# The gate-and-up product of an encoder trunk: seven block products in another order, two of them continued in PSUM, and weight parts made by pairs of row tiles

## The chip, the cores and the metric

The kernel runs on one core of a Trainium2 chip. Times are device microseconds of one launch of the whole program. Three runs of the kernel before gave 1506.62, 1507.06 and 1509.12 us; the median is 1507.06 us.

## The reference, cut to what matters

The reference is a trunk of two layers for 512 tokens with a model width of 1024. Each layer has a mixer and a SwiGLU feed-forward block with 2816 hidden columns, each followed by a residual and a LayerNorm. All of it is float32. The change touches only the first product of the feed-forward block, which is computed once in each of the two layers:

```
def swiglu_ffn(x, w_gate_up, w_down):
    gu = x @ w_gate_up                       # (512, 1024) @ (1024, 2 * 2816)
    gate, up = gu[..., :FFN_HIDDEN], gu[..., FFN_HIDDEN:]
    return (jax.nn.silu(gate) * up) @ w_down
```

## The kernel before, in words

A float32 operand is held in two parts, a high one (a rounded copy, type fp32r) and a low one (the operand less its high part). `split` (L185) makes them: ScalarE casts the high part (L186) and VectorE, or GpSimd where told, subtracts for the low part (L187). A product of two operands takes three matmuls: high by high (L180), high of x by low of the weights, and low of x by high of the weights (L181 and L182); `gemm3` issues them one behind the other. The profile writes the operands of a matmul as out<-moving or stationary names; "wl" is the weights' low part.

`ffn` (L1112) computes x @ w_gate_up by Winograd's form of Strassen's product. x^T is cut in halves of the tokens (256) and of the model's columns (512), w_gate_up in halves of its rows and in gate and up. Seven block products P1 to P7 take the place of eight. The blocks of x (P1 to P7's left operands) and their parts are made once, by `sink` (L1132), when the norm before hands over x^T; P1, P2, P4 and P7 take parts of x^T itself, P5, P6 and P3 take sums of its blocks from the tile S.

The hidden columns are worked in six groups, four of 512 columns and two of 384 (`GROUPS`, L35). For one group the weights are four blocks B11, B12 (gate and up of the upper rows), B21, B22 (of the lower rows), each of four row tiles of 128 rows. They are loaded by eight DMAs on SyncE's queue, one for a row tile with gate and up side by side (L1192, 512 KB). GpSimd makes the blocks' sums (`sub`, L1200): for P6, B11 <- B12 - B11 and T2 <- B22 - B11; for P5 the new B11 serves; for P7, B12 <- B22 - B12; for P4, T2 <- B21 - T2.

`product` (L1156) runs one block product for a group: for each of two pairs of row tiles it takes a set of places for parts (tags wh and wl, two sets), and for each row tile of the pair it calls `split` on that tile (128 x 512 or 128 x 384) and then six matmuls, three for each half of the block's tokens (u = 0, 1). So a product has 24 matmuls, four casts and four low parts, and ends in two PSUM banks. There are eight banks: four with tag g, one each with t and o, two with s for transposes; the products take g, g, and t with o in turn.

`step` (L1223) runs a product and takes its result out of PSUM. P1 is copied by ScalarE (s1, L1239). All others are added by VectorE (L1234): g = P2 + s1; u = P6 + s1; w = P5 + u; v = P7 + w; u = P7 + u; w = P3 + w; u = P4 + u. ScalarE applies silu to g (L1246) and to u (L1255), GpSimd multiplies w by g (L1252), and VectorE multiplies v by u (L1256). So w and v are the two token halves of the hidden layer; `turn` (L1258) transposes them on TensorE (L1263) into the rows of `hid`, which ScalarE copies from PSUM (L1264).

`work` (L1269) runs the groups one behind the other in the order P1 P2 P6 P5 P7 P3 P4. The transposes of a group come after P2 of the next one. The first product of group 1 (`first_product`, L1174) is taken ahead and stands behind P2 of group 0, since the second half of the tokens is still in the norm then. `LOW` (L954) says which engine makes the low parts of these three products: VectorE and GpSimd in turn for the first layer's P1, GpSimd for all in the second layer.

The order in which each engine gets its instructions isn't that of the program text alone: a planner hands each engine, by a model of the times, the earliest instruction in program order whose operands and places are ready. Each engine then runs its queue in that order.

What follows the product is the down projection (`down`, L1655, with `down_ln`), which is unchanged; it uses the same two sets wh and wl and the same buffers w for its weights.

## Time and profile before

| | |
|---|---|
| median of the runs | 1507.06 us (1506.62 to 1509.12) |
| profiled execution, its span | 1508.2 us |
| TensorE busy | 1390.2 us, 92% |
| VectorE busy | 1113.9 us, 74% |
| ScalarE busy | 646.3 us, 43% |
| GpSimd busy | 532.1 us, 35% |
| mean granted TensorE clock | 0.964 |

The profiled execution's own time is its span, from the first to the last instruction; nothing outside it is recorded. Engines are named PE (TensorE's matmuls), PEld (its weight loads), DVE (VectorE), ACT (ScalarE), POOL (GpSimd) and SP (SyncE). In a timeline, a start in us is followed by the time to the end of a run of like instructions; a bracket holds the idle time ahead of it and who ended it. Matmuls are pipelined: the start of one to the start of the next is their rate, while the duration shown holds the latency too.

### The profile page before, as it was taken

To read this page: it belongs to the slowest core of one execution; us is meant where nothing else is said; L and a number is where in the kernel's file an instruction comes from. 1 tells how busy PE (TensorE), PEld (TensorE's weight loads), DVE (VectorE), ACT (ScalarE), POOL (GpSimd) and SP (SyncE) were. 2 spreads that over 40 slices of the span, in tenths; PEclk is the share of its full clock that TensorE was granted. 3 is DMA by queue.
4 is the path that set the end of the run, shared out by engine and by line. 5 is a ranking of instruction groups with operands and counts; after the bars stand their busy time and mean duration, and the time that the engine had idled before them with its cause. 6 is when DMAs were issued, how large, how long until landed. Compare 5 with 4: busy or idle time off the path is not lost. (4 is left out here: it accounts for less than half of the span.)

```text
span 1508.2 us, 22040 instructions
## 1 busy us (share of the span) xinstructions
PE 1390.2 (92%) x8366; PEld 1090.2 (72%) x8366; DVE 1113.9 (74%) x1858; ACT 646.3 (43%) x1223; POOL 532.1 (35%) x422
## 2 busy tenths in 40 slices
PE   8989989999959888999999999999988988989997
PEld 4767767667737676788877877766666776888886
DVE  3688776446697889889556457988798788988456
ACT  5533233344334444445433246555433444455341
POOL 1433122131384576466501230000466377561000
PEclk9999999999979999999999999999999999999999
DMA  5212111203503203222233221111403212222222
GB/s 178 82 50 49 35 43 40 51 22 119 181 15 140 83 29 112 85 84 66 88 99 113 91 67 60 51 52 45 169 25 125 99 32 93 84 84 85 85 97 98
DMA packets 57051, 120.98 MB, mean 80 GB/s; under 512 B 19312, under 2 KB 20464, under 8 KB 56816
## 3 DMA queue, kind: packets, MB, share of 16 engines
q1 hardware_dynamic: 56416, 117.46, 23.4%
q10 hardware_dynamic: 528, 2.10, 0.4%
q8 instruction: 66, 1.08, 0.3%
q14 instruction: 41, 0.34, 0.1%
HBM read 116.58 MB, written 2.95 MB: 79 GB/s over the span
## 5 line engine op out<-in xcount | busy, mean ns | idle before, releaser
L187 DVE TENSOR_TENSOR wl<-w,wh 128x512 fp32r<-128x512 f32 (+3 forms) x289 | 270.5, 968 | 72.2 <-ACT wh L186 72.0
L186 ACT CAST wh<-w 128x512 fp32r<-128x512 f32 (+3 forms) x309 | 195.0, 665 | 205.6 <-PE ps_g L182 143.9
L181 PE MATMUL ps_g<-wl,xh 128*128 128x512 f32 (+1 forms) x432 | 174.9, 405 | 37.9 <-DVE wl L187 35.1
L208 POOL TENSOR_TENSOR wl<-w,wh 128x512 fp32r<-128x512 f32 x64 | 88.1, 1379 | 246.0 <-ACT wh L207 213.5
L180 PE MATMUL ps_g<-wh,xh 128*128 128x512 f32 (+1 forms) x432 | 170.3, 396 | 3.0 <-ACT wh L186 2.4
L182 PE MATMUL ps_g<-wh,xl 128*128 128x512 f32 (+1 forms) x432 | 170.2, 396 | 0.0
L1200 POOL TENSOR_TENSOR w<-w 128x512 f32<-128x512 f32 (+1 forms) x96 | 145.3, 1528 | 30.8 <-DVE wl L187 28.2
L181 PEld LDWEIGHTS ps_g<-wl,xh 128*128 128x128 f32 x432 | 85.9, 199 | 65.3 <-DVE wl L187 48.0
L180 PE MATMUL ps_g<-xh,wh 128*128 128x512 f32 (+2 forms) x296 | 117.2, 396 | 0.0
L187 DVE TENSOR_TENSOR wl<-tt,wh 128x512 fp32r<-128x512 f32 (+1 forms) x96 | 104.1, 1116 | 17.6 <-ACT wh L186 17.5
L181 PE MATMUL ps_g<-wl,ah 128*128 128x512 f32 x288 | 112.2, 391 | 2.9 <-DVE wl L187 2.9
L181 PE MATMUL ps_g<-xl,wh 128*128 128x512 f32 (+2 forms) x296 | 114.8, 388 | 0.0
L182 PE MATMUL ps_g<-xh,wl 128*128 128x512 f32 (+2 forms) x296 | 114.6, 387 | 0.0
L181 PE MATMUL ps_g<-wl,Sh 128*128 128x512 f32 (+1 forms) x288 | 110.5, 384 | 3.5 <-DVE wl L187 3.4
L180 PE MATMUL ps_g<-wh,Sh 128*128 128x512 f32 (+1 forms) x288 | 110.2, 385 | 3.3 <-ACT wh L186 3.3
L182 PE MATMUL ps_g<-wh,al 128*128 128x512 f32 x288 | 112.0, 390 | 0.0
L180 PE MATMUL ps_g<-wh,ah 128*128 128x512 f32 x288 | 110.8, 392 | 0.2
L182 PE MATMUL ps_g<-wh,Sl 128*128 128x512 f32 (+1 forms) x288 | 109.0, 378 | 0.0
L180 PEld LDWEIGHTS ps_g<-wh,xh 128*128 128x128 f32 x432 | 85.8, 199 | 18.2 <-ACT wh L186 2.6
L187 DVE TENSOR_TENSOR al<-hid,ah 128x512 fp32r<-128x512 f32 x72 | 50.3, 710 | 62.8 <-ACT ah L186 62.7
L182 PEld LDWEIGHTS ps_g<-wh,xl 128*128 128x128 f32 x432 | 86.4, 200 | 12.2
L187 POOL TENSOR_TENSOR wl<-w,wh 128x512 fp32r<-128x512 f32 (+1 forms) x20 | 32.8, 1656 | 176.0 <-ACT wh L186 176.0
(433 smaller groups left out, 3151.5 us busy)
## 6 DMA issues: line engine op xcount, KB each, us to landing
w<-in_w_gu SPq DMA_DIRECT2D x64, 512.0 KB
w<-in_w_dn SPq DMA_DIRECT2D x44, 512.0 KB
w<-in_w_even SPq DMA_DIRECT2D x48, 256.0 KB
w<-in_w_gu SPq DMA_DIRECT2D x32, 384.0 KB
w<-in_w_q SPq DMA_DIRECT2D x12, 384.0 KB
w<-in_w_eo SPq DMA_DIRECT2D x16, 256.0 KB
w<-in_w_mi SPq DMA_DIRECT2D x8, 512.0 KB
w<-in_w_mo SPq DMA_DIRECT2D x8, 512.0 KB
```

Source lines behind the costliest of these rows:

```text
L180: nc.tensor.matmul(out, lhsT=wh, rhs=xh, start=first, stop=False)
L181: nc.tensor.matmul(out, lhsT=wh, rhs=xl, start=False, stop=False)
L182: nc.tensor.matmul(out, lhsT=wl, rhs=xh, start=False, stop=last)
L186: c = nc.scalar.copy(h, src)
L187: (eng or nc.vector).tensor_tensor(l, in0=src, in1=h, op=ALU.subtract)
L208: nc.gpsimd.tensor_tensor(l, in0=w, in1=h, op=ALU.subtract)
L1200: nc.gpsimd.tensor_tensor(o, in0=a, in1=b, op=ALU.subtract)
```

## The change

The seven products of a group are no longer run one group at a time. P1 of a group (but group 1, whose P1 is still taken ahead, now between P1 and P2 of group 0) comes before P4 of the group before, and P2 after it. P2's matmuls go on in the banks of P1 (tags t and o) without clearing them, and P4's in those of P7 (two of the four banks g); so g = silu of those banks, and u + P7 is no more added by itself. Group 1's P2 has banks of its own. `product` calls `split` once for a pair of row tiles (128 x 1024, or 128 x 768) and issues all matmuls with the pair's high part, then those with its low part. In groups 0 to 3, but for the first three products, each third pair takes its parts from a third set, in the places of hid's tiles 4 and 5. The weights are loaded by blocks, four DMAs for each, one for a row tile's half (256 KB or 192 KB); the first block goes into the buffers w of the down projection, all others into four buffers of one block each. The scratch blocks of `sink` move from hid's tiles 3 and 4 to 2 and 3.

```diff
-LOW = ("PDPD", "DDDD", "DDDD"), ("PPPP", "PPPP", "PPPP")
+LOW = ("PD", "DD", "DD"), ("PP", "PP", "PP")
...
-    full = [{n: hid.row(12 + 4 * u + i).rearrange("p (k t) -> p k t", t=P) for i, n in enumerate(("P1", "P2", "P7", "P6"))} for u in range(2)]
+    full = [{n: hid.row(8 + 4 * u + i).rearrange("p (k t) -> p k t", t=P) for i, n in enumerate(("P1", "P2", "P7", "P6"))} for u in range(2)]
...
+    def parts(n, spare):
+        count[0] += 1
+        if spare and count[0] % 3 == 0:
+            if not third:
+                third.extend(hid.make(4 + r, "third", F32R).rearrange("p m s -> p (m s)") for r in range(2))
+            hl = third
+        else:
+            hl = [g.wp.tile([P, 1024], F32R, tag=t, name=t, bufs=2) for t in ("wh", "wl")]
+        return [x[:, :2 * n].rearrange("p (q n) -> p q n", q=2) for x in hl]
+
+    def banks(chain):
+        return [g.pp.tile([P, S], F32, tag=t, name="ps_g", bufs=4 if t == "g" else 1) for t in ("to" if chain else "gg")]
+
+    def product(name, n, source, acc, first=True, spare=True, eng="DD"):
+        A_ = A[name]
         for k2 in range(2):
-            h, l = (g.wp.tile([P, 1024], F32R, tag=t, name=t, bufs=2) for t in ("wh", "wl"))
-            for q in range(2):
-                k = 2 * k2 + q
-                qs = slice(512 * q, 512 * q + n)
-                split(nc, h[:, qs], l[:, qs], source(k), nc.gpsimd if eng[k] == "P" else nc.vector)
-                for u in range(2):
-                    us = slice(P * u, P * u + P)
-                    gemm3(nc, acc[u], A_[0][:, k, us], A_[1][:, k, us], h[:, qs], l[:, qs], k == 0, k == 3)
-        return acc
+            h, l = parts(n, spare)
+            split(nc, h, l, source(k2), nc.gpsimd if eng[k2] == "P" else nc.vector)
+            for b, w in enumerate((h, l)):
+                for q in range(2):
+                    k = 2 * k2 + q
+                    for u in range(2):
+                        for a in range(2 - b):
+                            nc.tensor.matmul(acc[u][:, :n], lhsT=A_[a][:, k, P * u:P * u + P], rhs=w[:, q], start=first and k + a + b == 0,
+                                             stop=k + b == 4, skip_group_check=True)
...
+        def load(r, q):
+            if (r, q) == (0, 0) and j != 1:
+                b = [g.wp.tile([P, 1024], F32, tag="w", name="w", bufs=2)[:, :2 * n].rearrange("p (k n) -> p k n", k=2) for k2 in range(2)]
+            else:
+                t = tp.tile([P, 2048], F32, tag="raw", name="raw", bufs=4)[:, :4 * n].rearrange("p (k n) -> p k n", k=4)
+                b = [t[:, 0:2], t[:, 2:4]]
+            for k in range(4):
+                nc.sync.dma_start(b[k // 2][:, k % 2], w[4 * r + k][:, q * n:q * n + n])
+            out[r, q] = b
...
+            chained = {"P2": "P1", "P4": "P7"}.get(name)
+            if chained in acc:
+                acc[name] = acc[chained]
+            else:
+                acc[name] = banks(name in ("P1", "P2") and not (j == 1 and name == "P1"))
+                chained = None
+            product(name, n, lambda k2: source(name, k2), acc[name], chained is None, spare, eng)
...
+                elif name == "P2":
+                    if chained:
+                        d.g = E("g")[:, :n]
+                        nc.scalar.activation(d.g, acc[name][u][:, :n], AF.Silu)
+                    else:
+                        d.g = add(name, u, d.s1)
+                        nc.scalar.activation(d.g, d.g, AF.Silu)
...
                 elif name == "P7":
-                    d.v = add("v", d.w)
-                    add(d.u2, d.u2)
+                    d.v = add(name, u, d.w)
...
+        for j, x in enumerate(gs):
+            more = j < 4
+            if j != 1:
+                x.step("P1", more and j > 0, LOW[i][0] if j == 0 else "DD")
+            if j == 0:
+                gs[1].step("P1", False, LOW[i][1])
+            else:
+                gs[j - 1].turn(0)
+                gs[j - 1].step("P4", more)
+                for r, q in ((1, 0), (0, 1), (1, 1)):
+                    x.load(r, q)
+            x.step("P2", more and j > 0, LOW[i][2] if j == 0 else "DD")
+            if j:
+                gs[j - 1].turn(1)
+            x.step("P6", more)
+            x.step("P5", more)
+            if 0 < j < last:
+                gs[j + 1].load(0, 0)
+            x.step("P7", more)
+            x.step("P3", more)
+        gs[last].step("P4", False)
```

## Rows read from the trace of the kernel before

**Rows 1.** The page's first part: busy time, share of the span, instructions.

```profile
span 1508.2 us, 22040 instructions
...
PE 1390.2 (92%) x8366; PEld 1090.2 (72%) x8366; DVE 1113.9 (74%) x1858; ACT 646.3 (43%) x1223; POOL 532.1 (35%) x422
```

**Rows 2.** Windows: length, busy PE, PEld, DVE, ACT, POOL, clock, DMA share, GB/s.

```profile
425.39:464.87 39.48, 26.41 (x81) 19.32 (x82) 34.88 (x33) 15.95 (x29) 25.82 (x17) 0.68 0.04 14
464.87:703.80 238.93, 218.78 (x1013) 184.48 (x1012) 206.91 (x247) 109.38 (x210) 140.59 (x100) 0.96 0.24 83
1111.79:1138.34 26.55, 17.67 (x73) 12.78 (x72) 26.48 (x29) 15.47 (x28) 19.21 (x13) 0.90 0.11 39
1138.34:1376.32 237.98, 218.14 (x1010) 184.80 (x1011) 206.31 (x247) 107.55 (x206) 140.01 (x96) 0.95 0.23 80
530.27:577.40 47.13, 43.34 (x185) 35.06 (x184) 40.62 (x45) 21.26 (x38) 29.15 (x18) 0.93 0.25 91
```

**Rows 3.** Windows of PE alone: length, busy PE, granted clock, DMA share, GB/s.

```profile
519.38:530.26 10.88, 10.88 (x49) 1.00 0.92 331
691.31:703.78 12.47, 12.47 (x73) 1.00 0.06 18
543.48:549.95 6.47, 6.46 (x16) 0.53 0.00 0
```

**Rows 4.** Timeline of PE, 451 to 554.

```profile
451.25 0.80 PE L181 MATMUL ps_g<-wl,xh 128*128 128x512 f32 x1 [5.54 <-DVE wl L187]
...
539.83 0.39 PE L180 MATMUL ps_g<-wh,xh 128*128 128x512 f32 x1
543.49 0.80 PE L181 MATMUL ps_g<-wl,xh 128*128 128x512 f32 x1 [3.28 <-DVE wl L187]
...
553.06 1.03 PE L1263 MATMUL ps_s<-cst,w 128*128 128x128 f32 x8
553.85 0.48 PE L180 MATMUL ps_g<-wh,Sh 128*128 128x512 f32 x1
```

**Rows 5.** Waits in 464 to 703.8: us in total, times, longest.

```profile
PEld ps_g L181 <- DVE wl L187: 23.3, 22, 3.8
...
PE ps_g L181 <- DVE wl L187: 15.2, 7, 3.4
```

**Rows 6.** Timeline of POOL, 530 to 562.

```profile
530.56 3.00 POOL L1252 TENSOR_TENSOR w<-w,g 128x512 f32<-128x512 f32 x2 [19.49 <-DVE w L1234]
...
537.80 3.42 POOL L1200 TENSOR_TENSOR w<-w 128x512 f32<-128x512 f32 x2
...
554.71 6.47 POOL L1200 TENSOR_TENSOR tt<-w,tt 128x512 f32<-128x512 f32 x4
```

**Rows 7.** Timeline of DVE, 534 to 643.

```profile
534.03 1.28 DVE L187 TENSOR_TENSOR wl<-w,wh 128x512 fp32r<-128x512 f32 x2
...
538.32 3.45 DVE L1256 TENSOR_TENSOR v<-v,u 128x512 f32<-128x512 f32 x2
541.69 5.12 DVE L187 TENSOR_TENSOR wl<-w,wh 128x512 fp32r<-128x512 f32 x3
...
636.09 6.47 DVE L187 TENSOR_TENSOR wl<-w,wh 128x384 fp32r<-128x384 f32 x5
```

**Rows 8.** Groups by form, DVE, 720 to 790: busy, mean ns, idle before.

```profile
L187 DVE TENSOR_TENSOR wl<-w,wh 128x1024 fp32r<-128x1024 f32 x12 | 14.8, 1230 | 2.6 <-ACT wh L186 2.6
```

**Rows 9.** Groups by form, ACT, 720 to 790.

```profile
L186 ACT CAST wh<-w 128x1024 fp32r<-128x1024 f32 x12 | 12.6, 1046 | 0.0
```

**Rows 10.** Groups by form, DVE, 464.87 to 703.8.

```profile
L1234 DVE TENSOR_TENSOR g<-ps_g,s 128x512 f32<-128x512 f32 x6 | 3.8, 676 | 0.0
```

**Rows 11.** Line 187 in the whole trace: ns least, median, most; forms.

```profile
L187 DVE TENSOR_TENSOR wl<-w,wh x289: 424/692/2349, 438.5 to 1469.1; 128x512 fp32r<-128x512 f32 x73, 128x384 fp32r<-128x384 f32 x40, 128x1024 fp32r<-128x1024 f32 x23, 128x768 fp32r<-128x768 f32 x8
...
L187 POOL TENSOR_TENSOR wl<-w,wh x20: 1271/1725/2612, 426.1 to 1128.5; 128x512 fp32r<-128x512 f32 x18, 128x1024 fp32r<-128x1024 f32 x2
```

**Rows 12.** Timeline of SP, 1085 to 1095.

```profile
1087.65 4.28 SPq L1178 DMA_DIRECT2D w<-in_w_gu  x4
```

More of the change, by code (lines that the diff above doesn't have):

```diff
@@ L175, with of @@
 class Ctx:
-    pass
+    @classmethod
+    def of(cls, **k):
+        c = cls()
+        c.__dict__.update(k)
+        return c
 def gemm3(nc, out, wh, wl, xh, xl, first, last):
@@ L1174, in first_product @@
-    def first_product(j):
-        r = [g.wp.tile([P, 1024], F32, tag="w", name="w", bufs=2) for k2 in range(2)]
-        for k in range(4):
-            nc.sync.dma_start(r[k // 2][:, 512 * (k % 2):512 * (k % 2) + 512], g.I[f"w_gu{i}{j}"][k][:, :512])
-        acc = product(A["P1"], 512, lambda k: r[k // 2][:, 512 * (k % 2):512 * (k % 2) + 512], LOW[i][2])
-        out = []
-        for u in range(2):
-            out.append(E("s1"))
-            nc.scalar.copy(out[u], acc[u])
-        return out
@@ L1186, in group @@
-    def group(j, s1=None):
+    third = []
+    count = [0]
+    def parts(n, spare):
[9 more added lines that the diff above has]
+        return [g.pp.tile([P, S], F32, tag=t, name="ps_g", bufs=4 if t == "g" else 1) for t in ("to" if chain else "gg")]
@@ L1187, in group, with blocks @@
+    def blocks(j):
         c, n = GROUPS[j]
         w = g.I[f"w_gu{i}{j}"]
[L1189 to L1196 removed]
@@ L1197, in group @@
-        T2 = [tt[:, k * n:k * n + n] for k in range(4)]
+        out = {}
+        def load(r, q):
[7 more added lines that the diff above has]
+            out[r, q] = b
@@ L1199, in sub, with group, source @@
+        return out, load
+    def group(j):
+        c, n = GROUPS[j]
+        B, load = blocks(j)
+        e = [Ctx(), Ctx()]
+        acc, T2 = {}, []
         def sub(o, a, b):
             nc.gpsimd.tensor_tensor(o, in0=a, in1=b, op=ALU.subtract)
-        def source(name, k):
-            if name == "P1":
-                return B11[k]
-            if name == "P2":
-                return B21[k]
-            if name == "P3":
-                return B22[k]
-            if name == "P6":
-                sub(B11[k], B12[k], B11[k])
-                sub(T2[k], B22[k], B11[k])
-                return T2[k]
+        def source(name, k2):
+            B11, B12, B21, B22 = (B[r, q][k2] if (r, q) in B else None for r in range(2) for q in range(2))
+            if name in ("P1", "P2", "P3"):
+                return {"P1": B11, "P2": B21, "P3": B22}[name]
+            if name == "P6":
+                if not T2:
+                    tt = g.cp.tile([P, 2, D], F32, tag="gb", name="tt").rearrange("p a b -> p (a b)")
+                    T2.extend(tt[:, 2 * k * n:2 * k * n + 2 * n].rearrange("p (k n) -> p k n", k=2) for k in range(2))
+                sub(B11, B12, B11)
+                sub(T2[k2], B22, B11)
+                return T2[k2]
@@ L1213, in source @@
             if name == "P5":
-                return B11[k]
+                return B11
             if name == "P7":
-                sub(B12[k], B22[k], B12[k])
-                return B12[k]
-            sub(T2[k], B21[k], T2[k])
-            return T2[k]
-        e = [Ctx(), Ctx()]
-        def step(name):
-            if s1 and name == "P1":
-                for u in range(2):
-                    e[u].s1 = s1[u]
-                return
-            acc = product(A[name], n, lambda k: source(name, k), LOW[i][int(name == "P2")] if j == 0 and name in ("P1", "P2") else "DDDD")
+                sub(B12, B22, B12)
@@ new lines, in source, with add, step @@
+                return B12
+            sub(T2[k2], B21, T2[k2])
+            return T2[k2]
+        def add(name, u, x, o=None):
+            o = E(name)[:, :n] if o is None else o
+            nc.vector.tensor_tensor(o, in0=acc[name][u][:, :n], in1=x, op=ALU.add)
+            return o
+        def step(name, spare=True, eng="DD"):
+            chained = {"P2": "P1", "P4": "P7"}.get(name)
[5 more added lines that the diff above has]
+            product(name, n, lambda k2: source(name, k2), acc[name], chained is None, spare, eng)
@@ L1266, in group @@
[L1266 to L1283 removed]
+                    add(name, u, d.u, d.u)
@@ new lines, in step, with turn @@
+                    nc.scalar.activation(d.u, d.u, AF.Silu)
+                    nc.vector.tensor_tensor(d.v, in0=d.v, in1=d.u, op=ALU.mult)
+        def turn(half):
+            for u in range(2):
+                y = (e[u].w, e[u].v)[half]
+                t = 2 * half + u
+                p = g.pp.tile([P, S], F32, tag="s", name="ps_s", bufs=2)[:, :n]
+                for m in range(n // P):
+                    nc.tensor.transpose(out=p[:, m * P:(m + 1) * P], in_=y[:, m * P:(m + 1) * P], identity=g.C("ident"))
+                nc.scalar.copy(hid.tile(j)[:, :, t * P:(t + 1) * P], p.rearrange("p (m t) -> p m t", t=P))
@@ new lines, in group @@
+        return Ctx.of(load=load, step=step, turn=turn)
+    def work():
+        gs = [group(j) for j in range(len(GROUPS))]
+        for r, q in ((0, 0), (1, 0), (0, 1), (1, 1)):
+            gs[0].load(r, q)
+        gs[1].load(0, 0)
+        last = len(gs) - 1
+        for j, x in enumerate(gs):
[19 more added lines that the diff above has]
+        gs[last].step("P4", False)
+        return [lambda h=h: gs[last].turn(h) for h in range(2)]
```

58 lines of the change are left out of this document (6 added, 52 removed).

## The prediction

> **What bounds the kernel now.** I read the page first: TensorE is busy 92% of the span, VectorE 74% [rows 1]. A busy TensorE is not yet TensorE at its rate, so I went by stages. The change touches only the gate-and-up product, which runs twice: from 425.39 us (its first matmul) to 703.80 us, and from 1111.79 us to 1376.32 us [rows 2]. Each run has a start, in which the first three products (P1 and P2 of group 0, P1 of group 1) stand beside the end of the norm before, and a long rest.
>
> The bare rate comes from stretches without a stall [rows 3]: 48 matmuls of 512 columns in 10.88 us, 0.2267 us each; 72 of 384 columns in 12.47 us, 0.1732 each (the x counts there also hold a neighbour that overlaps the edge). Eight transposes take 0.79 us (553.06 to 553.85) [rows 4], 0.10 each. The rest of a run has 25 products of 24 matmuls of 512 columns (600), 14 of 384 columns (336) and 76 transposes: 136.0 + 58.2 + 7.5 = 201.7 us. It took 238.93 and 237.98 us [rows 2]. So 37.2 and 36.3 us, together 73.5 us, are lost there.
>
> Who takes them: the longest waits of TensorE are for VectorE's low parts [rows 5]. The timeline shows one: at 539.83 the matmul of a high part runs, then TensorE idles 3.28 us until a low part is there [rows 4], and the matmuls that follow run at the lower clock (granted 0.53 from 543.48 to 549.95, where 0.43 us pass from one to the next) [rows 3]: 15 of them by 0.20 is another 3 us. It comes once in each of the five changes of group. For one group, 47.13 us [rows 2] stand against 168 x 0.2267 + 16 x 0.10 = 39.7, so 7.4 is lost.
>
> Why VectorE is late: GpSimd starts on its subtractions at 530.56 and goes on to 561.2 [rows 6]. Beside it two low parts that took 1.28 us take 3.41 (three in 5.12) [rows 7], and VectorE's product v x u, 3.45 us for two [rows 7], stands ahead of them in its queue. Before and after that stretch it has time, but only two sets of parts exist, so it can't run ahead.
>
> **The change, part by part.**
>
> *Low parts' products last.* Eight products of the pair's high part come ahead of its four low ones: the low part is due 8 x 0.2267 = 1.8 us after the high one. Instructions and weight loads stay the same in number; nothing is added.
>
> *Parts for two row tiles at once.* 28 subtractions of 512 columns in a group become 14 of 1024. One of 1024 takes 1.23 us undisturbed [rows 8], two of 512 1.28 [rows 7]: 0.05 less, under 1 us a group. The cast becomes one of 1.05 us [rows 9]; the first matmul now waits for that in place of a half as long, which costs nothing while a set is made ahead.
>
> *A third set of parts* (groups 0 to 3): two pairs can wait where one did.
>
> *P2 onto P1, P4 onto P7.* VectorE loses the adds for g (2 x 0.68 [rows 10]; not in group 1, whose P2 opens its own banks) and the second adds of P7 to u, alike in shape: 2.7 us a group. The copy s1 stays, beside P4's products that now lie between P1 and P2, so the new wait of P2's first matmul for that copy (two of 0.6 us at most, by the cast that is longer) is over by then. P4 waits for the add of v from P7, a whole product earlier. The pair of banks is held for longer, and P6 of the next group takes them after P4's adds, with P2 (5.4 us) between.
>
> *The order.* P1 of the next group stands between P3 and P4, P4 before P2. VectorE's adds of u, and v x u, now fall beside P2, whose parts can lie ready.
>
> What it makes of the late low parts: let T be P3's end. Before, P4, P1 and P2 follow (5.44 us each, 24 x 0.2267), and the last quarter of P2 starts at T + 2.75 x 5.44 = T + 15.0. By then VectorE must do five pairs of low parts and, for w and u, four adds from PSUM (0.68 each, as the row of g's [rows 10]) and v x u: 4 x 0.68 + 3.45 = 6.2 us. At the undisturbed 1.28 a pair this is 12.6, at the disturbed 3.42 23.3: between 2.4 to spare and 8.3 short. It fell short by 3.3, at 0.53 of the way. After, with P1's two pairs ready at T, six remain, those of P4, P2 and P6. The last is due when P6's second half has gone through its high products: P1, P4 and P2 (16.3), two turns of 0.8, half of P6 (2.7) and eight high products (1.8), T + 22.4. Bounds: 6 x 1.23 + 6.2 = 13.6 (8.8 to spare) and 6 x 3.42 + 6.2 = 26.7 (4.3 short). At 0.53 of the way it is 1.9 to spare, so the stall goes. A pair of 1024 beside GpSimd is in the trace at 2.35 at most [rows 11], inside these bounds.
>
> The Trainium skill ("SBUF — State Buffer", Who interferes with whom) has a rule against wide instructions here: the port pair that VectorE and GpSimd share is held for a whole instruction, so a part that comes behind a subtraction waits for all of it. GpSimd's of 1024 would hold it up to 2.61 us [rows 11], and six pairs at 2.61 + 1.23 would be 2.5 us longer than at 3.42. By that rule, with GpSimd at work throughout, a change of group would stay 6.8 short, about as much as now, and the time would be that of the last rival, 1506; at 0.53 of the way it has 0.5 to spare, and the sum stands. The trace agrees with the rule only in part: adds from PSUM keep their 0.68 [rows 10], but a part beside a subtraction takes 1.71 [rows 7], less than the 1.27 and 0.64 of the two one after the other [rows 11, 7].
>
> In groups 4 and 5 (384 columns) there are only two sets: seven pairs. Disturbed, five parts took 6.47 us [rows 7], 2.6 a pair; undisturbed I scale 1.23 by 384/512, 0.92. With 4.8 us of adds (6.2 x 0.77) that is 11.2 to 23.0, due at T + 17.5: on the edge at 0.53 (17.5).
>
> So of the ten changes of group I leave 1.2 us each to the six of 512 columns (waits of about that size remain at turns) and 2.5 each to the four of 384, which stay on the edge and may keep a clock loss: 17 us. The gain is 73.5 - 17 = 56.5.
>
> *The start.* 72 matmuls (16.3 us) take 39.48 and 26.55 us [rows 2], with VectorE busy for 34.88 and 26.48 of them; TensorE's longest wait, 5.54 us up to 451.25, is again for a low part [rows 4]. The change takes 1.4 us of adds from VectorE. Against it GpSimd's first low part is a pair, 2.61 for 1.28, and the blocks come through more and smaller loads, the first into buffers that in the second run the earlier projection frees (loads there at 1087.65 [rows 12], 24 us ahead of use). SP's queue then holds all later blocks behind it: 4 MB at 331 GB/s [rows 3] are 13 us, so P1 of group 1 has its block at about 1105. Bounds: 5 us better (the adds, and three low parts' grace) to 5 worse (the pair on GpSimd, late blocks) a run. I take 1 better, the adds' row less a little: 2 in all.
>
> *Loads in the rest.* 16 of 256 KB for 8 of 512 KB, the same bytes; 4 MB a group are 13 us of 40. The queue is in order, but each block's buffer comes free by P7 or earlier (P3 for one of group 1), if P4's subtractions stay as early as now (third rival). Nothing.
>
> Sum: 1508.2 - 56.5 - 2 = 1449.7 for the profiled execution. The median of the runs, 1507.06, lies 1.1 below that span, so about 1449; I say 1450.
>
> **Rivals.**
>
> *Everything goes:* no stall, no fall of the clock, the starts 3 us better each: 1508.2 - 73.5 - 6 = 1429. For it: the spare of 1.9 us, and that VectorE has 40.62 us of work in 47.13 [rows 2], some 37 after. Against: 37 in 40 leaves little, and the 384 groups are on the edge.
>
> *The shared work of VectorE and GpSimd binds:* a third set can't be filled, since VectorE has no spare time ahead of T either, and only the removed work counts: 2 x 0.68 of g and 6 x 0.05 by wide parts in the stretch, 1.7 us in each of ten changes. 1508.2 - 17 = 1491. For it: beside GpSimd a product's four parts take 6.8 us and TensorE 5.44. Against: in those 47.13 us VectorE is idle for 6.5 [rows 2], and that is ahead of T.
>
> *Slower: blocks come late.* The second column block of a group takes the buffer of the group before's third operand B21, which P4's subtractions release. In the trace these run at 554.71, long ahead of P3's end, and GpSimd's product with g waits 19.49 us behind them for P3 [rows 6]. If they now land behind that product, they end at T + 0.3 + 3.0 + 6.5 = T + 10, the two blocks (2.1 MB) arrive by T + 16.5, and four subtractions of 2 x 1.71 end near T + 27: P6's second half, due at T + 20.6, starts at T + 28, 7.3 late, 10 with the clock, three quarters of it at 384 columns. Five changes: 3 x 10 + 2 x 7.5 = 45 against 37 lost now, 1508 + 2 x 8 = 1524. It decides from 7.4 us a change upwards. For it: GpSimd's queue is in order. Against: their operands are ready early, now and after.
>
> *No change that can be told:* the stall only moves from P1 to P6, at its old price; the starts' 2 us are all: 1506.
>
> **Chances.** The forecast (1436 to 1474) 0.52; everything goes 0.15; shared work 0.16; slower 0.12; no change 0.05. A measurement here tells about 0.2%, 3 us, from nothing. Faster 0.83, same 0.05, slower 0.12. For 8 in 10 the range leaves out the slower case, no change and the far end below: 1426 to 1500; the forecast's own is 1436 to 1474.
>
> **What would show it.** The waits for low parts in the first rest, 23.3 us of the weight loads and 15.2 of the matmuls [rows 5], fall to a third; granted clock of the rests rises from 0.95 to 0.98 or more; each rest near 210 us; the g adds gone from VectorE; GpSimd's P4 subtractions still ahead of its product with g. Wrong, if TensorE then waits at P6 for high parts made from GpSimd's results (slower), if the rests stay above 225 us (shared work), or if the starts differ by over 5 us.

## The result, and the profile after

The changed kernel took 1533.90 us (median of 4 runs, 1529.89 to 1535.26) where the kernel before took 1507.34 beside it: 1.0166 times as long, 95% interval 1.015 to 1.0182. Forecast were 1450 us and a faster kernel; it is slower by 26.6 us and lies outside the range. The profiled execution spans 1528.1 us, 19.9 more than before.

The first part of its page; [rows 1] has the same lines of before:

```profile
span 1528.1 us, 21779 instructions
...
PE 1385.7 (91%) x8366; PEld 1096.4 (72%) x8366; DVE 1037.9 (68%) x1653; ACT 631.8 (41%) x1055; POOL 496.2 (32%) x319
```

VectorE has 76 us less to do, ScalarE and GpSimd have less too, and the time is longer. So no engine's amount of work explains it. Next the stages, as in [rows 2]: the first run's start and rest, the second's start and rest, and the first 8.4 us after one stop (columns: length, busy time of PE, PEld, DVE, ACT and POOL, granted clock, DMA share, GB/s).

```profile
425.46:467.19 41.73, 26.49 (x80) 19.60 (x81) 34.10 (x26) 14.91 (x22) 21.89 (x10) 0.66 0.04 13
467.19:709.94 242.75, 214.12 (x1014) 185.41 (x1012) 165.37 (x149) 103.64 (x134) 126.84 (x59) 0.94 0.24 77
1114.57:1147.84 33.27, 24.11 (x97) 18.79 (x97) 32.15 (x36) 12.90 (x21) 23.29 (x12) 0.85 0.03 7
1147.84:1396.10 248.26, 215.27 (x1014) 185.96 (x1012) 172.41 (x154) 105.45 (x137) 127.30 (x56) 0.93 0.24 77
...
547.61:556.00 8.39, 8.28 (x30) 6.69 (x31) 1.22 (x1) 2.36 (x4) 5.84 (x3) 0.71 0.01 2
```

[rows 2] let the second rest of before start too late, at 1138.34: the first two matmuls of that P6 ran 3.1 us earlier, ahead of a wait for a low part. From the timeline of PE of before:

```profile
1135.25 0.73 PE L180 MATMUL ps_g<-wh,Sh 128*128 128x512 f32 x2 [3.31 <-ACT wh L186]
```

and its second rest from there, as a window:

```profile
1135.25:1376.32 241.07, 218.88 (x1012) 185.09 (x1013) 209.40 (x251) 109.06 (x209) 141.29 (x97) 0.95 0.23 79
```

So the rests are 3.8 and 7.2 us longer than before. The first P6 comes 2.3 us later; from the end of the first run to the second's P6 it is 437.9 us (709.94 to 1147.84) after 431.5 (703.80 to 1135.25). Together 19.8 of the 19.9.

TensorE's waits in the first rest (us in total, times, longest):

```profile
ACT hid L1284 <- PE ps_s L1283: 32.7, 11, 12.4
PEld ps_s L1283 <- POOL P L1271: 32.4, 10, 10.4
...
PE ps_s L1283 <- POOL P L1271: 28.3, 7, 10.0
```

The waits for VectorE's low parts, 23.3 and 15.2 us in [rows 5], are gone: the last two lines are the only ones that the view shows for TensorE. In their place the transposes (L1283) wait for GpSimd's product of w with g (L1271). The timeline of PE shows one such stop, that between groups 1 and 2 (start, length, in brackets the idle time before and its releaser):

```profile
540.50 1.07 PE L1187 MATMUL ps_g<-wl,xh 128*128 128x512 f32 x4
547.61 2.34 PE L1283 MATMUL ps_s<-cst,P 128*128 128x128 f32 x8 [6.04 <-POOL P L1271]
549.60 0.78 PE L1187 MATMUL ps_g<-wh,xh 128*128 128x512 f32 x1
```

P1 of group 2 has ended and P4 of group 1 has its parts, but the transposes of w stand ahead of P4, and TensorE's queue is in order. The clock is granted at 0.71 over the 8.39 us from there. VectorE had w ready long before. In its timeline the third line is the add of P3, which gives w; the first two are the low parts of the two pairs of group 2's P1, made before it; the last three are low parts of products that come later:

```profile
531.70 1.21 DVE L191 TENSOR_TENSOR third<-w,third 128x1024 fp32r<-128x1024 f32 x1
533.62 2.85 DVE L191 TENSOR_TENSOR wl<-w,wh 128x1024 fp32r<-128x1024 f32 x1 [0.71 <-ACT wh L190]
536.40 1.27 DVE L1238 TENSOR_TENSOR P<-ps_g,P 128x512 f32<-128x512 f32 x2
537.60 2.22 DVE L191 TENSOR_TENSOR wl<-tt,wh 128x1024 fp32r<-128x1024 f32 x1
539.75 3.41 DVE L191 TENSOR_TENSOR third<-tt,third 128x1024 fp32r<-128x1024 f32 x1
543.08 3.35 DVE L191 TENSOR_TENSOR wl<-raw,wh 128x1024 fp32r<-128x1024 f32 x1
```

GpSimd's timeline says why the product comes late:

```profile
532.99 2.40 POOL L1215 TENSOR_TENSOR w<-raw,w 128x1024 f32<-128x1024 f32 x1 [15.81 <-DVE third L191]
535.47 3.26 POOL L1215 TENSOR_TENSOR raw<-raw 128x1024 f32<-128x1024 f32 x1
538.70 3.37 POOL L1215 TENSOR_TENSOR w<-raw,w 128x1024 f32<-128x1024 f32 x1
542.15 3.20 POOL L1215 TENSOR_TENSOR raw<-raw 128x1024 f32<-128x1024 f32 x1
545.31 3.46 POOL L1271 TENSOR_TENSOR P<-P,P 128x512 f32<-128x512 f32 x2
```

w is ready at 537.67 (536.40 + 1.27); the product starts at 545.31, 7.6 us later, because four subtractions of the next group (for P6 and P7) stand ahead of it in GpSimd's queue. The first overwrites the block that P1's first pair is made from, and the second what the first has read: they became ready when that pair's low part was done, at 532.91 (531.70 + 1.21). The other two became ready with the second pair's, at 536.47 (533.62 + 2.85), still ahead of w, since with a third set each pair gets its place one pair earlier. What was to be VectorE's lead let GpSimd's next work start ahead of what was due. Before, GpSimd stood idle 19.49 us up to the product and began it at 530.56 [rows 6].

### The profile page after: what moved, and what is told of

The parts are those of the page before. It is cut to its first block, busy times and chain, and to the rows that moved or that the text cites. A ratio compares the mean times of both kernels' runs of the same rounds, so it can differ in the third digit from the quotient of the medians.

```text
span 1528.1 us, 21779 instructions
## 1 busy us (share of the span) xinstructions
PE 1385.7 (91%) x8366; PEld 1096.4 (72%) x8366; DVE 1037.9 (68%) x1653; ACT 631.8 (41%) x1055; POOL 496.2 (32%) x319
## 3 DMA queue, kind: packets, MB, share of 16 engines
q8 instruction: 66, 1.08, 0.3%
## 4 chain that ended last, share of the span: by engine, by line
PE 44%; POOL 8%; DVE 7%; issue 6%; DMA 3%; ACT 1%; SPq 1%; POOLq 0%; DVEq 0%; ACTq 0%
PE ps_g L1187 12%; PE ps_g L185 8%; PE ps_g L184 8%; PE ps_g L186 8%; PE ps_s L1573 2%; POOL w L1215 2%; POOL P L1271 2%; POOL raw L1215 2%; PE ps_o L1602 2%; DMA w<-in_w_gu 2%; POOL tt L1215 1%; PE ps_t L1589 1%; DVE wl L191 1%; PE ps_s L1283 1%; DVE x L1014 1%
## 5 line engine op out<-in xcount | busy, mean ns | idle before, releaser
L191 DVE TENSOR_TENSOR wl<-w,wh 128x1024 fp32r<-128x1024 f32 (+2 forms) x92 | 115.6, 1257 | 36.0 <-ACT wh L190 35.6
L1187 PE MATMUL ps_g<-wh,xh 128*128 128x512 f32 (+1 forms) x312 | 125.1, 402 | 8.5 <-ACT wh L190 8.5
L190 ACT CAST wh<-w 128x1024 fp32r<-128x1024 f32 (+3 forms) x101 | 95.5, 949 | 87.5 <-PE ps_g L185 36.0
L1187 PE MATMUL ps_g<-wh,xl 128*128 128x512 f32 (+1 forms) x312 | 123.3, 395 | 0.0
L191 DVE TENSOR_TENSOR wl<-raw,wh 128x1024 fp32r<-128x1024 f32 (+1 forms) x60 | 76.9, 1283 | 68.2 <-ACT wh L190 42.6
L190 ACT CAST wh<-raw 128x1024 fp32r<-128x1024 f32 (+1 forms) x64 | 62.1, 971 | 104.4 <-PE ps_g L1187 94.1
L191 DVE TENSOR_TENSOR al<-hid,ah 128x512 fp32r<-128x512 f32 x72 | 50.3, 710 | 62.8 <-ACT ah L190 62.6
L1215 POOL TENSOR_TENSOR tt<-raw,tt 128x1024 f32<-128x1024 f32 (+1 forms) x24 | 61.2, 2551 | 90.5 <-DVE wl L191 76.2
L1187 PE MATMUL ps_g<-wl,xh 128*128 128x512 f32 (+1 forms) x312 | 82.5, 387 | 6.5 <-DVE wl L191 6.5
L1215 POOL TENSOR_TENSOR w<-raw,w 128x1024 f32<-128x1024 f32 (+1 forms) x20 | 49.2, 2458 | 116.9 <-DVE wl L191 85.0
L1283 PE MATMUL ps_s<-cst,P 128*128 128x128 f32 x176 | 33.7, 332 | 58.4 <-POOL P L1271 57.6
L1215 POOL TENSOR_TENSOR raw<-raw 128x1024 f32<-128x1024 f32 (+1 forms) x28 | 79.6, 2852 | 20.2 <-DMA raw<-in_w_gu 18.8
```

The lines of the kernel that those rows point to most:

```text
L190: c = nc.scalar.copy(h, src)
L191: (eng or nc.vector).tensor_tensor(l, in0=src, in1=h, op=ALU.subtract)
L1187: nc.tensor.matmul(acc[u][:, :n], lhsT=A_[a][:, k, P * u:P * u + P], rhs=w[:, q], start=first and k + a + b == 0, stop=k + b == 4, skip_gr ...
L1215: nc.gpsimd.tensor_tensor(o, in0=a, in1=b, op=ALU.subtract)
L1283: nc.tensor.transpose(out=p[:, m * P:(m + 1) * P], in_=y[:, m * P:(m + 1) * P], identity=g.C("ident"))
```

## The experiments

Times are medians; the kernel before ran beside each on the same chip (1506.2 to 1507.5 us). Behind each time stands its ratio to the kernel before, with the 95% interval. "w x g" is the product on line 1271. "Theory" and "rival" are the cases of the expectation above each result. Three questions came one after the other: is it the product's lateness; what makes it late; what were the forecast's other gains worth?

**The product on VectorE.**

```
e1:  - nc.gpsimd.tensor_tensor(d.w, in0=d.w, in1=d.g, op=ALU.mult)
     + nc.vector.tensor_tensor(d.w, in0=d.w, in1=d.g, op=ALU.mult)
```

> Only the product of w with g (line 1271) goes from GpSimd to VectorE; nothing is left out. Theory 1 (that product stands in GpSimd's queue behind the next group's subtractions, the transposes of w wait for it, and TensorE's queue with them): the 28 to 29 us of matmul waits on it in each feed-forward block and the half-clock stretches behind them go, about 40 us a block; near 1450 us. Theory 2 (P4 and P2 themselves come late, by blocks or by PSUM banks; the transposes only show it): the stall moves to P4's or P2's first matmul and the time stays within 10 us of 1530.

1487.83 us, 0.9875 [0.9851, 0.9899]: 46 us off the changed kernel, so the late product is what makes the change slower, but it stays 38 us above the forecast.

**The transposes of w later**, so that the product has time.

```
e2:  - gs[j - 1].turn(0)                  (ahead of P4)
     + gs[j - 1].turn(0)                  (behind P2, ahead of turn(1))
```

> Only the place of the transposes of w is changed: behind P2 of the next group, beside those of v; the product with g stays on GpSimd, as late as in the changed kernel (some 13 us behind P3's end). Theory 1: TensorE's queue holds P4 and P2 (10.9 us) ahead of them and no longer stands still, near 1455 us, the change of groups 0 to 1 keeping a rest (the product is 16 us late there and only 10.9 of matmuls lie ahead). Theory 2: P4 or P2 stall in their place, within 10 us of 1530.

1510.69 us, 1.0026 [1.0011, 1.0041]: between the two expectations, half as much as e1. The wait moves: TensorE's transposes now wait for the copies to hid (L1284), which stand on ScalarE behind casts of T2 that wait for GpSimd's subtractions (21.0 us in the first rest).

**The blocks of the second run's start**, and both. In the change the first block of every group but group 1 goes into the buffers w; e3 turns this round between groups 0 and 1 of the second run.

```
e3:  - if (r, q) == (0, 0) and j != 1:          e4: e1 and e3
     + if (r, q) == (0, 0) and j != 1 - i:
```

> Only in the second layer: group 0's first weight block goes into the block buffers, and group 1's first block into the buffers w that the projection before frees late. Theory: the second start is 6 us longer because that first block came at 1092 us, so that P1's parts and P6's subtractions fall beside the norm's tiles on VectorE; 1530 - 6 = 1524. Rival (the scratch blocks of x^T in hid's tile 2 wait for the projection's parked parts): no change, 1530.

> The product with g on VectorE and the second layer's first blocks as in the run before it: if the two causes are independent, their gains add: about 1444 us, by theory 1 and the first theory of the start.

1528.58 us, 1.0145 [1.0115, 1.0175], and 1486.50, 0.9864 [0.9841, 0.9887]. Against the changed kernel and e1 the intervals overlap: no effect on the time that can be told.

**The product first in GpSimd's queue.** A dependency without a wait orders the next group's subtractions behind it:

```
e5:  + x = nc.gpsimd.tensor_tensor(o, in0=a, in1=b, op=ALU.subtract)
     + [behind(g, x, y) for y in gate[:2 * j]]      (gate: the products w x g so far)
```

> The product w x g stays on GpSimd, but the next group's subtractions are ordered behind it in GpSimd's queue; nothing else changes. Theory 1 (the changed kernel loses only because the planner put those subtractions ahead of w x g in an in-order queue): the product starts when P3's adds are there and ends some 5 us later, as P1's 5.4 us end, so the transposes of w wait under 1 us. The four subtractions for P6 (4 x 3.2 = 13 us) then end about 20 us after P3, against a need at some 19.5, so P6 is just on time: 1450 to 1475 us. Rival (GpSimd has too much to do around a change of group, and whatever comes last is late): the wait goes to the high parts of P6's second half and to the casts behind them on ScalarE, 1495 to 1515 us.

1532.64 us, 1.0175 [1.0152, 1.0198]: no gain. The rival had the mechanism, but the loss is larger than its range. Between groups 1 and 2 the transposes of w follow P1 without a gap, but those of v, ahead of P6, wait 5.6 us. Four timelines of e5 show the chain. ACT, the cast of T2 and the silu of u:

```profile
556.33 1.05 ACT L190 CAST third<-tt 128x1024 fp32r<-128x1024 f32 x1 [7.31 <-POOL tt L1215]
557.28 1.14 ACT L1274 ACTIVATE P<-P 128x512 f32<-128x512 f32 x2
```

DVE, the low part of that cast and v x u:

```profile
557.41 2.31 DVE L191 TENSOR_TENSOR third<-tt,third 128x1024 fp32r<-128x1024 f32 x1 [4.53 <-ACT third L190]
559.64 5.59 DVE L1275 TENSOR_TENSOR P<-P,P 128x512 f32<-128x512 f32 x2
```

PE, the transposes of v:

```profile
562.62 1.09 PE L1283 MATMUL ps_s<-cst,P 128*128 128x128 f32 x4 [5.62 <-DVE P L1275]
```

POOL, w x g and the subtractions that make T2:

```profile
540.41 3.52 POOL L1271 TENSOR_TENSOR P<-P,P 128x512 f32<-128x512 f32 x2 [19.86 <-DVE P L1238]
...
553.91 4.72 POOL L1215 TENSOR_TENSOR tt<-raw,w 128x1024 f32<-128x1024 f32 x2
```

The product is on time (540.41), T2 is now late (from 553.91), ScalarE's cast of T2 waits 7.31 us with the silu of u (L1274) behind it, VectorE's low part waits for that cast with v x u (L1275) behind it, and the transposes of v wait for that. One late result goes through the heads of three in-order queues.

**Both sets of transposes later, with the product on VectorE.**

```
e6 (on e1):  - gs[j - 1].turn(0)                  (ahead of P4)
             + gs[j - 1].turn(0)                  (behind P2)
             - gs[j - 1].turn(1)                  (behind P2)
             + gs[j - 1].turn(1)                  (behind P6)
```

> The version with w x g on VectorE, and both sets of transposes one place later: those of w behind P2 instead of ahead of P4, those of v behind P6 instead of ahead of it. Theory 1 (what the VectorE version still loses against the forecast are TensorE's waits at the transposes, 20 us of gaps in the first rest and as many in the second, with the clock behind them): 1445 to 1465 us. Rival (as when the transposes of w alone were moved: the wait goes on to the copies behind the casts in ScalarE's queue): within 10 us of 1488.

1484.60 us, 0.9855 [0.9829, 0.9881]: the rival; the stops move from the transposes to low parts (10.4 us in the first rest).

**Two sets of parts; low parts not last.**

```
e7 (on e1):  - more = j < 4          e8 (on e1): the loop over high and low
             + more = False                      inside those over q and u
```

> The version with w x g on VectorE, and without the third set of parts (two sets everywhere). Theory 1 (the third set is what lets VectorE run ahead, as the forecast's step on the due times has it): in the ten changes of group six of 512 columns lose their spare of 2.7 us and more, the low parts' stalls come back in part: 1500 to 1515 us. Rival (VectorE is ahead anyway once its adds are fewer and the order of products is changed): within 5 us of 1488.

> The version with w x g on VectorE, but a low part's products follow those of its high part row tile by row tile and bank by bank, as in the kernel before, and not after all eight high ones. Theory 1 (that low parts come last buys 1.4 us of grace, which the changes of group use): 1495 to 1510 us. Rival (the third set already keeps the low parts ahead, so their place is free): within 4 us of 1488.

e7: 1473.69 us, 0.9795 [0.9769, 0.9822], against both expectations: without the third set it is 14 us faster. This version beats both kernels. e8: 1492.70, 0.9912 [0.9887, 0.9936]: by the medians low parts last are worth 4.9 us, between the two expectations, but its interval overlaps that of e1.

**The order, the third set, and a control.** e9 is the changed kernel in the old order, e11 the kernel before with w x g on VectorE.

```
e9:   - gs[j - 1].turn(0)                         (ahead of P4)
      - gs[j - 1].step("P4", more)                (behind the next P1)
      + x.step("P4", more)                        (behind P3)
      + gs[j - 1].turn(0)                         (behind the next P2, ahead of turn(1))
e10:  - more = j < 4
      + more = False
e11:  - nc.gpsimd.tensor_tensor(d.w, in0=d.w, in1=d.g, op=ALU.mult)
      + nc.vector.tensor_tensor(d.w, in0=d.w, in1=d.g, op=ALU.mult)
e12:  e7 with e6's places of the transposes
```

e9 keeps the change's order of the first three products and its loads by blocks.

> The changed kernel with one part undone: the order. P4 follows P3 again and both sets of transposes stand behind the next group's P2; w x g stays on GpSimd, and the pairs, the low parts last, the third set and the sums in PSUM stay. Theory 1 (the new order is what loses: it wants w x g 5.4 us after P3, where the old one wants it 16 us after): the waits at the transposes go and the other parts' gain shows, 1455 to 1475 us. Rival (GpSimd and VectorE have too much to do around a change, whatever the order): 1500 to 1530 us.

> The changed kernel with only the third set of parts undone (two sets everywhere); w x g stays on GpSimd, the order stays new. Theory 1 (GpSimd's queue is what holds TensorE up, and the sets have nothing to do with it): within 6 us of 1534. Rival (the third set lets casts and low parts be issued too far ahead, and they block what is due, on GpSimd's queue too): 1505 to 1522 us, as two sets gained 14 us with the product on VectorE.

> A control: the kernel before the change with w x g on VectorE in place of GpSimd, nothing else. Theory 1 (the product on VectorE helps the changed kernel only because its new order needs the product early): here the product has time and VectorE is the engine that is late, so 3.5 to 4.5 us more for it in each change cost 10 to 35 us: 1517 to 1542 us. Rival (GpSimd is overloaded in both kernels, and moving work off it gains in both): 1475 to 1500 us.

> The version with w x g on VectorE and two sets of parts, with both sets of transposes one place later (those of w behind P2, those of v behind P6). Theory 1 (what it still loses are waits of 1.4 to 1.6 us at the turns, twice a change, with the clock behind some of them): 1452 to 1464 us. Rival (VectorE's products then only land on the low parts of P2 and P6 in its queue): 1470 to 1480 us, no gain over 1474.

e9: 1515.26, 1.0056 [1.004, 1.0072], in the rival's range: the order alone isn't it. e10: 1495.23, 0.9928 [0.9902, 0.9954], the rival's way and beyond it: undoing the third set alone takes 38.7 us off and makes the change faster than before. e11: 1502.16, 0.9966 [0.9946, 0.9986], nearer the rival: the same move is worth 5 us in the kernel before, so some 41 of e1's 46 belong to what the change did to that product. e12: 1474.53, 0.9793 [0.977, 0.9815]: nothing over e7. GpSimd's timeline of e10:

```profile
532.47 2.41 POOL L1215 TENSOR_TENSOR w<-raw,w 128x1024 f32<-128x1024 f32 x1 [15.76 <-DVE wl L191]
534.95 3.26 POOL L1215 TENSOR_TENSOR raw<-raw 128x1024 f32<-128x1024 f32 x1
538.17 4.45 POOL L1271 TENSOR_TENSOR P<-P,P 128x512 f32<-128x512 f32 x2
```

With two sets each pair gets its place one pair later. In VectorE's timeline of e10 the low part of P1's second pair comes behind the add of P3, and not ahead of it:

```profile
533.48 1.29 DVE L1238 TENSOR_TENSOR P<-ps_g,P 128x512 f32<-128x512 f32 x2 [1.09 <-PE ps_g L1187]
534.68 1.27 DVE L191 TENSOR_TENSOR wl<-w,wh 128x1024 fp32r<-128x1024 f32 x1
```

So two subtractions stand ahead of the product in place of four, and TensorE's wait for it falls to this (first rest):

```profile
PE ps_s L1283 <- POOL P L1271: 14.8, 8, 5.2
```

**What each part is worth without the third set.**

```
e13:          e9 with more = False
e14 (on e7):  - chained = {"P2": "P1", "P4": "P7"}.get(name)
              + chained = None
              + add(name, u, d.u, d.u)            (in P7, for P4's sum; every third product in banks "to")
e15 (on e10): - nc.gpsimd.tensor_tensor(d.w, in0=d.w, in1=d.g, op=ALU.mult)
              + (nc.gpsimd, nc.vector)[u].tensor_tensor(d.w, in0=d.w, in1=d.g, op=ALU.mult)
e16 (on e7):  - split(nc, h, l, source(k2), ...)
              + for q in range(2): split(nc, h[:, q], l[:, q], b[:, q], ...)      (b = source(k2))
```

> The changed kernel with two parts undone: the third set and the order (P4 behind P3, both sets of transposes behind the next group's P2); w x g on GpSimd. With three sets undoing the order took 19 us off, with the new order undoing the third set took 39 off. Theory 1 (the new order makes w x g due early and so loses on its own, whatever the sets): 1465 to 1485 us, below the 1495 of the new order with two sets. Rival (the new order gives VectorE and GpSimd time and gains on its own; it lost only with the third set, which brings the subtractions ahead of w x g): 1498 to 1512 us.

> The version with w x g on VectorE and two sets, without the sums in PSUM: P2 and P4 open banks of their own (every third product in the other pair, as in the kernel before), and VectorE adds g from s1 and P7 to u again, 4 adds of 0.68 us a group, 2.7 us. Theory 1 (VectorE's work around a change of group is what is left, so its adds count): 1485 to 1500 us. Rival (those adds fall where VectorE waits anyway): within 5 us of 1474.

> Two sets, and w x g shared: the first 128 tokens' product on GpSimd, the second's on VectorE. With two sets the whole on GpSimd took 1495, the whole on VectorE 1474. Theory 1 (GpSimd's queue is what holds the transposes, by two subtractions ahead of the product, some 5.7 us): the first product is as late as before and one half of the wait stays, 1485 to 1495 us. Rival (what counts is how much work either engine has): 1455 to 1468 us.

> The version with w x g on VectorE and two sets, but each pair's parts made by two casts and two subtractions of 512 columns (384 in the last groups) for one of 1024, as in the kernel before. Theory 1 (the pair only saves 0.05 us each): within 5 us of 1474. Rival (a wide subtraction on VectorE holds GpSimd up and the other way round, so narrow ones let both through): 1455 to 1466 us. Other rival (the start of 0.07 to 0.2 us that each instruction has on ScalarE and VectorE counts twice, where both are on the path): 1480 to 1495 us.

e13: 1515.29, 1.0042 [1.0019, 1.0065], just above the rival's range: the new order gains 20 us with two sets (e13 to e10) and loses 19 with three (e9 to the changed kernel). In the old order the third set changes nothing (e9, e13). In the old order low parts stop TensorE again, 4.05 us at 553.04 on e13's timeline of PE:

```profile
553.04 0.79 PE L1187 MATMUL ps_g<-wl,xh 128*128 128x512 f32 x1 [4.05 <-DVE wl L191]
```

e14: 1481.77, 0.9833 [0.9802, 0.9864]: the sums in PSUM are worth 8.1 us, between the expectations. e15: 1485.25, 0.984 [0.981, 0.987]: theory 1, just halfway. e16: 1483.94, 0.9833 [0.9804, 0.9861]: the wide parts are worth 10.3 us; neither theory 1 nor the first rival, but the second rival's size. The two sizes are differences of medians against e7; every run of e14 and e16 is slower than every run of e7, but the intervals of the ratios overlap, so they are rough. e16 leaves GpSimd's subtractions wide. Groups by form in the first rest (busy us, mean ns, idle before), e16:

```profile
L190 ACT CAST wh<-raw 128x512 fp32r<-128x512 f32 x48 | 27.4, 619 | 37.1 <-PE ps_g L1189 33.3 <-DVE wl L191 2.2 <-DVE P L1240 1.6
...
L191 DVE TENSOR_TENSOR wl<-raw,wh 128x512 fp32r<-128x512 f32 x48 | 45.0, 973 | 3.5 <-ACT wh L190 2.1 <-ACT hid L1286 1.4
```

and e7:

```profile
L190 ACT CAST wh<-raw 128x1024 fp32r<-128x1024 f32 x24 | 25.3, 1055 | 37.7 <-PE ps_g L1187 37.7
...
L191 DVE TENSOR_TENSOR wl<-raw,wh 128x1024 fp32r<-128x1024 f32 x24 | 36.9, 1539 | 4.8 <-ACT wh L190 4.6
```

A pair of these blocks costs VectorE 2 x 0.973 = 1.95 us in narrow pieces and 1.54 in a wide one, ScalarE 1.24 and 1.06.

**By what way the third set acts.** e17 is e10 with e5's dependency. e18 is e5 (three sets) with the first subtraction for P6 and the first for P7 left free, which gives GpSimd's queue e10's order from the second group on.

```
e18 (on e5):  - sub(B11, B12, B11)                - sub(B12, B22, B12)
              + sub(B11, B12, B11, k2 == 0)       + sub(B12, B22, B12, k2 == 0)      (True: no dependency)
```

> Two sets, w x g on GpSimd, and in GpSimd's queue w x g stands ahead of all of the next group's subtractions (with two sets alone, two of them stood ahead: 1495 us). Theory 1 (one queue, two dues: whichever goes last is late): the transposes of w wait no more, but the subtractions for P6 end some 6 us later, and the casts that wait for them hold up ScalarE: 1495 to 1525 us. Rival (the two subtractions ahead are all that two sets still lose): 1468 to 1480 us.

> The changed kernel with its third set, w x g on GpSimd, but GpSimd's queue in the order that the version with two sets has from the second group on: two of the next group's subtractions ahead of w x g, the other ones behind it (three sets alone: four to six ahead, 1534 us; two sets: 1495 us). Theory 1 (the third set costs only through the order that the planner then gives GpSimd's queue): 1488 to 1502 us. Rival (it costs through the casts and low parts that ScalarE and VectorE then do ahead of what is due): 1515 to 1535 us.

e17: 1499.52, 0.9952 [0.993, 0.9973]: theory 1, and no gain over e10; one queue with two dues, and whichever is last is late. e18: 1505.27, 0.9982 [0.9964, 1.0001], just above theory 1's range and well below the rival's: GpSimd's order is 29 of the 39 us. Its waits of PE in 467 to 700 us hold the rest:

```profile
PE ps_s L1283 <- DVE P L1275: 10.4, 7, 2.1
PE ps_s L1283 <- POOL P L1271: 7.6, 6, 1.5
```

The second line is no worse than e10's 14.8. The first is new (1.2 us in e10): v x u stands behind low parts that the third set let VectorE's queue take earlier.

| us | w x g on GpSimd | w x g on VectorE |
|---|---|---|
| new order, three sets | 1533.9 (the change) | 1487.8 (e1) |
| new order, two sets | 1495.2 (e10) | 1473.7 (e7) |
| old order, three sets | 1515.3 (e9) | not run |
| old order, two sets | 1515.3 (e13) | not run |

## Why the prediction was wrong, point by point

- **What bounds the kernel** held: the rests lose to VectorE's late low parts, and these can go. They do.
- **Low parts last, pairs, sums in PSUM:** right in sign. Low parts last gave some 4.9 us (e8), near the noise. The pairs were mis-sized: priced at 0.05 us each from two undisturbed rows [rows 7, 8], they saved 0.41 each on VectorE and 0.18 on ScalarE in the groups shown, some 10.3 us in the time (e16). The sums' adds, 14 of 0.68 and 8 of 0.55 us in a run, 28 us of VectorE in both, came to 8.1 in the time (e14).
- **VectorE beside GpSimd** was read too mildly. The prediction held that a low part beside a subtraction takes less than the two one after the other. In the timelines of after above each low part that begins beside a subtraction ends 1.08 or 1.09 us behind that subtraction's end: 536.47 after 535.39, 539.82 after 538.73, 543.16 after 542.07, 546.43 after 545.35. Alone it takes 1.21. So it waits for the whole rest of the subtraction and saves only some 0.13 us, and the prediction's own 1.71 for a narrow part, against 1.27 and 0.64, is such a wait less 0.2. Its bound of 3.42 for a pair held (3.41 at 539.75). Adds with one input in PSUM keep 0.684 us (before 0.676, [rows 10]). The Trainium skill ("SBUF — State Buffer", Who interferes with whom) calls the shared port pair an exclusive lock and has a VectorE instruction with two SBUF inputs, as a low part is, contend with a GpSimd one that reads SBUF; the trace agrees. What the prediction drew from it, that wide parts fare worse, did not come out: e16's narrow ones are slower. No term of the sum hung on it.

```profile
L1238 DVE TENSOR_TENSOR P<-ps_g,P 128x512 f32<-128x512 f32 x32 | 20.6, 684 | 14.1 <-PE ps_g L1187 14.1
```

- **The order: this step failed.** It priced the turn of w at 0.8 us, with "P1 of the next group" ahead of it as cover, and took w x g to be ready. The due time was worked out for VectorE's parts alone. GpSimd's product had gone from a due of T + 16.3 (behind P4, P1 and P2) to T + 5.4, and its place in GpSimd's queue was taken from before [rows 6], where it ran first. In the trace of after it starts 7.6 us after w is ready in the change shown, and each change of group of the first rest has such a stop (10.0, 6.0, 6.0, 3.6 and 1.1 us at the first transposes). With two sets the order does gain, 20 us.
- **A third set: wrong in sign.** "Two pairs can wait where one did" was counted as a lead and nothing else. The lead is there, but it frees both halves of B11 before w is there, and with them four subtractions (12.2 us by the rows above) that the planner then puts ahead of w x g. In the new order it costs 39 us with the product on GpSimd and 14 with it on VectorE; in the old order, tried with the product on GpSimd, nothing. So neither part is wrong by itself: the loss comes of the two together.
- **The third rival** ("blocks come late", 1524, chance 0.12) had the engine, the in-order queue and nearly the time, but the wrong instructions: P4's subtractions do stay early; P6's and P7's of the next group were never placed against the product. The step "Loads in the rest" asked about GpSimd's order only for the loads.
- **What would show it:** the waits for low parts fell by more than forecast, and the clock fell to 0.94 and 0.93 where 0.98 was forecast, which goes with the new stops: behind them matmuls run at the lower clock, as behind the old ones [rows 3]. Of the signs of being wrong, rests above 225 us came true, and a start that differs by over 5 us, the second's; a wait at P6 for high parts made from GpSimd's results did not.
- **The starts**, forecast 2 us better together, are 8.8 worse: 2.3 up to the first P6 and 6.4 from the end of the first run to the second's P6. The latter took 431.5 us before and 431.4 in e11; the nine versions with the product on GpSimd take 435.8 to 438.5, the eight with it on VectorE 430.7 to 436.5. In the change TensorE waits 11.9 us there for VectorE's tiles of the norm (L1014, 1060 to 1148 us), before 5.6; in e3 6.5, but 3.5 after 0.3 for low parts of the projection ahead (L191), and its stretch is only 2.2 us shorter. So the term "1 better" for a start was mis-sized in the second, 6.4 worse; whether the loads by blocks, the wide parts or the order of the first three products make VectorE late there is open, since no run undid each by itself. In the profiles the starts are also what makes the old order slower than the kernel before: both rests of e13 together are 5.7 us shorter than before, the ways to the two P6 11.0 longer.
- **The forecast's size** is partly met by e7, whose rests (windows as above) are:

```profile
466.51:684.30 217.79, 207.54 (x1014) 179.41 (x1012) 176.79 (x161) 104.03 (x135) 128.99 (x68) 0.99 0.27 88
1118.20:1338.40 220.20, 208.68 (x1014) 180.16 (x1012) 179.93 (x164) 103.97 (x135) 115.73 (x42) 0.98 0.27 87
```

That is 438.0 against a bare 403.4 (twice the prediction's 201.7): 34.6 us lost in place of 76.6 before and 17 in the forecast. The prediction had 73.5 for before, since it took the second rest 3.1 us too short. What is left there is spread over low parts and both products (first rest):

```profile
PE ps_g L1187 <- DVE wl L191: 4.3, 4, 1.2
PE ps_s L1283 <- DVE P L1271: 3.2, 2, 2.1
PE ps_s L1283 <- DVE P L1275: 2.8, 3, 1.1
```

## What to carry to other kernels

When an order is changed, list every consumer that moves ahead, find its producer on each engine, and write that producer's new due time beside what can stand ahead of it in that engine's queue; an idle engine on the page is no promise that the queue is free then. More buffers are not free: they let later work become ready sooner, and where a planner fills in-order queues that work can end up ahead of what is due, so a deeper buffer is tried by itself. Two parts of a change can each gain or cost nothing alone and lose together, so they are measured one by one before they are judged.

## What the runs showed of the hardware that was not expected

VectorE and GpSimd shut each other out, instruction by instruction, where both have two inputs in SBUF. In the trace of after, from 460 to 710 us, 19 low parts of 1024 columns on VectorE began while such an instruction ran on GpSimd. All ended 1.08 to 1.09 us behind it, whether 0.2 or 2.3 us of it were left. The other way round, the 15 subtractions of 1024 columns that began while such an instruction ran on VectorE ended 2.20 to 2.27 us behind it; alone they take 2.33 to 2.39. With narrow parts (e16, same stretch) the 35 of VectorE's of 512 columns that began beside GpSimd's ended 0.55 to 0.56 us behind. Adds with one input in PSUM went on beside GpSimd at 0.67 to 0.69 us.

With this the effect of the width can be understood. Beside GpSimd's subtractions a low part of 1024 columns takes less than two of 512 by 0.41 us, where undisturbed rows gave 0.05: in two pieces a pair can be shut out twice, in one piece once. GpSimd's own subtractions go the other way, since what they wait for is longer. Groups by form in the first rest, e7 with wide parts:

```profile
L1215 POOL TENSOR_TENSOR raw<-raw 128x1024 f32<-128x1024 f32 x8 | 24.3, 3054 | 12.8 <-DMA raw<-in_w_gu 12.5
```

and e16 with narrow ones:

```profile
L1217 POOL TENSOR_TENSOR raw<-raw 128x1024 f32<-128x1024 f32 x8 | 21.4, 2688 | 14.4 <-DMA raw<-in_w_gu 14.1
```

Each takes 3.05 us beside wide parts and 2.69 beside narrow ones, so with the width the delay goes from one of the two engines to the other. How much of the 10.3 us between e16 and e7 is this, and how much the start of twice as many instructions, was not tried by itself.
